# Hymba block on one core: keys turned on VectorE, one cluster for the last Gram blocks, stores and loads queued behind the weights

## The chip, the core and the metric

The kernel runs on one core of a Trainium2 chip. The metric is the device time of one execution in microseconds. A core has five engines that work side by side, each through its own list of instructions in order: TensorE (PE in the profile; its weight loads are shown apart as PEld), VectorE (DVE), ScalarE (ACT), GpSimd (POOL) and SyncE (SP). SyncE does no arithmetic here; it issues the transfers between DRAM and on-chip memory, one after the other, and a transfer that has to wait for data holds up all transfers behind it. An instruction that needs a result of another engine waits for a semaphore.

## The reference

The input `x` is 512 tokens of 2048 values in float32; 16 meta tokens stand ahead of them (528 rows in all). One layer is computed:

```
hn = rmsnorm(h);  P = hn @ w_in                       # 2048 -> 8320 columns
r, k, v, g_r, wl, al = token shift of the first 4224 columns (16 heads x 64)
decay = exp(-exp(-softplus(-(w0 + tanh(wl) @ w_lora_up)) - 0.5))
a  = sigmoid(a0 + al @ a_lora_up)
kk = k * k_k, each head's vector divided by its norm
k  = k * (1 + (a - 1) * k_a);   b = kk * a
S_t = S_{t-1} diag(decay_t) - (S_{t-1} kk_t) b_t^T + v_t k_t^T      # per head, 64 x 64
y_t = S_t r_t
y_a = (groupnorm(y) + sum(r * k * r_k) * v) * silu(g_r)
y_b = B * conv3(C * h) * silu(g_c)                     # the other 4096 columns
out = rmsnorm(h + concat(y_a, y_b) @ w_out), without the meta rows
```

## The kernel before, in words

**The projection.** Weights and activations are each split into a rounded part and a rest (`xh`, `xl`; `wh`, `wl`), and three products of them are summed (`steps`, line 315): `ps_k`, `ps_r`, `ps_v`, `ps_g`, `ps_C`, `ps_h`, `ps_B`, `ps_gc` are the groups of the profile. One tile of 128 columns ("a main") takes 16 x 3 matmuls for each of two ranges of tokens, or for all 512 tokens at once (B and gc). Weights arrive in blocks of 128 x 1024 (`wr`, three buffers, `prefetch`); ScalarE rounds each half (line 126) and VectorE, or GpSimd for the second half, forms the rest (line 127); a half is called a quarter of a main's weights here, as four make one main.

**Pairs of heads.** The 16 heads are worked in 8 pairs. The order of mains is: lora, then for each two pairs k, r, v, k, r, v, g, g, and a C, h, B, gc of the convolution; four more sets C, h, B, gc come at the end. The program of TensorE is written out by hand: `mains()` yields one projection matmul at a time, `fill(ns)` lets so many nanoseconds of them pass, `until(what, i)` all of them up to a named main, and between them stand the small matmuls of the pairs. `FW` holds the lengths of these fills. VectorE, ScalarE, GpSimd and SyncE are put in order by the tile scheduler when the kernel is built, by its own priorities (`high_priority`, `ahead()`); `issue_after` forbids a transfer to be placed ahead of a named other one.

**One pair** (`prepare(i)`): after its keys (`shift_full`, line 343) `lora_up` (lines 540 to 546) loads the pair's low-rank weights (`lur`), ScalarE rounds them (`luh`) and VectorE forms the rest (`lul`, line 545). 1062 ns of projection later `low_rank` (lines 521 and 522) multiplies by both parts, for the decay (`tz`) and for a (`ta`). From these come scaled keys `bk`, and `ar` with the scaled removal key and receptance; r is projected; after a fill (`gram` or `gram_b`) the Gram products of 9 chunks of 64 tokens follow on TensorE (line 625): eight chunks, a fill `gram2`, the ninth chunk, and 16 transposes of `bk` by TensorE (line 655) that ScalarE copies to `bt`; a fill `gram3`; then four matmuls that sum the squares of the keys (`n2`, line 666) and two that sum the bonus (`zb`, line 670). The norms go to DRAM (`sn`), as does a part of the Gram blocks (`sg`); `stash` stores the operands of the recurrence to DRAM (`opd`: `ar`, `gt`, `bt`, `vs`). `d` and `nd` are read back in another layout (line 697, 698), and VectorE inverts 72 blocks of 16 x 16 by 33 instructions (lines 701 to 734), called the solve below. The result goes to DRAM (`sx`) and comes back as `xT`, `xo` (`load_inverse`); both are put off by `later(ns, ...)`, which runs a function once so much projection has passed, behind the last weight's transfer. v follows: bonus times v is stored (`rbd`), v is turned (`vs`) and stored by 8 transfers.

**Two pairs** (`invert`): after a fill (`solve`), the inverses of 16 are joined to those of 64 on TensorE, and `xT` is stored.

**The recurrence** (`recur`): 9 chunks in turn; each loads its operands (`ct`, 16 buffers), and runs three clusters of small matmuls with fills between: `rz` (line 889), `z` and then `zs` (line 939: the change of the state) with `zy` (line 943: the outputs). It runs beside the last mains. Then `split_mix` splits what goes into the output projection (`o`, line 1070), which ends the kernel.

The lines that the change touches are 40 to 46 (`FW`), 420 (`mixd`), 540 to 546, 566, 621 to 673, 685 to 698, 749 to 757, 858 to 863, 921 and 939.

Of the kernel before, what the change touches and what calls it, by code (L numbers as in the profile page):

```python
# [40 lines left out]


FW = dict(
    evac=34, start=1062, lora=2200, gram=8000, gram_b=13500, gram2=4800, gram3=3500, misc=2000, v=2000, vt=1000, solve=22500, solve_first=26000,
    tr=3200, lev=3000, cp=4200, out=1500, begin=17000, p=2900, u=2900, s=5200, last=3700, mix=2600,
)

# [29 lines left out]
def hymba_kernel(ctx: ExitStack, tc: tile.TileContext, xt, xtok, w_in, w_out, pv, lup, cst, msk, gf, out):  # L77
# [299 lines left out]
    def use(what, i, ps):  # L377
        if what == "lora":
            use_lora(ps)
        elif what in ("k", "v"):  # L380
            t = cq.tile([P, LP], F32, tag=what, name=f"{what}{i}")
            nc.gpsimd.memset(t[:, META:CH], 0.0)
            shift_full(ps, tile_of[what] + i, f"{what}{i}", padded(t))
            got[what, i] = t
        elif what in ("r", "g"):
            t = cq.tile([P, SEQ], F32, tag=f"r{i % 2}" if what == "r" else "g", name=f"{what}{i}")
            shift_real(ps, tile_of[what] + i, f"{what}{i}", t)
            if what == "g":
                gate(t, f"r{i}")
                later(6000, lambda: nc.sync.dma_start(gated[i], t))  # L390
            got[what, i] = t
        elif what == "C":
            u = tm(f"u{i}")
            scaled(TAIL, ps, u, 14)
            got[what, i] = u
        elif what == "h":
            u = got["C", i]
            hh = tm(f"hh{i}")
            scaled(TAIL, ps, hh, 14)
            n = SEQ + 2  # L400
            nc.gpsimd.tensor_tensor(out=u[:, 0:n], in0=u[:, 0:n], in1=hh[:, 0:n], op=ALU.mult)
            cv = tp.tile([P, SEQ], F32, tag="cw", name=f"cv{i}")
            nc.scalar.activation(cv, u[:, 0:SEQ], AF.Copy, scale=col(V_CW, i))
            for j in (1, 2):
                nc.vector.scalar_tensor_tensor(
                    out=cv, in0=u[:, j : j + SEQ], scalar=col(V_CW, 8 * j + i), in1=cv, op0=ALU.mult, op1=ALU.add
                )
            got[what, i] = cv
        elif what == "B":
            cv = got["h", i]  # L410
            b = tm(f"b{i}")[:, 0:SEQ]
            scaled(REAL, ps, b, META)
            nc.gpsimd.tensor_tensor(out=cv, in0=cv, in1=b, op=ALU.mult)
        else:
            cv = got["h", i]
            g = tm(f"gc{i}")[:, 0:SEQ]
            scaled(REAL, ps, g, META)
            gate(g, f"c{i}")
            nc.vector.scalar_tensor_tensor(out=cv, in0=cv, scalar=0.5, in1=g, op0=ALU.mult, op1=ALU.mult)
            nc.sync.dma_start(mixd[8 + i], cv)  # L420
        ready.add((what, i))

    ready = set()
# [115 lines left out]
    def lora_up(i):  # L539
        raw = cq.tile([P, 2, P], F32, tag="lur", name=f"lur{i}")  # L540
        hi = cq.tile([P, 2, P], F32R, tag="luh", name=f"luh{i}")
        lo = cq.tile([P, 2, P], F32R, tag="lul", name=f"lul{i}")
        nc.sync.dma_start(raw, lup[i])
        nc.scalar.copy(hi, raw)
        nc.vector.tensor_tensor(out=lo, in0=raw, in1=hi.bitcast(F32), op=ALU.subtract)
        return hi, lo
# [17 lines left out]
        )  # L564

    def stash(i, src, o, n, row=0, rows_n=P, c0=0, cn=NCH, step=1):
        nc.sync.dma_start(spot(i, row, rows_n, c0, cn, step, o, n), src)

    def prepare(i):
        p = i % 2  # L570
# [47 lines left out]
        fill(FW["gram_b" if p else "gram"])  # L618

        gt = cq.tile([P, 2, NCH, P], F32, tag=f"gt{p}", name=f"gt{i}")  # L620
        bt = cq.tile([P, 2, NCH - 1, CH], F32, tag="bt", name=f"bt{i}")

        def gram(z, c, c0):
            for h, hs, ho in heads:
# [22 lines left out]
        masked(za, 0, 4)  # L647
        masked(zc, 4, 8)
        fill(FW["gram2"])
        ze = [pi.tile([P, 1, P], F32, tag=("misc", "ser")[h], name=f"g{i}_8_{h}") for h in range(2)]  # L650
        zz = [pz.tile([P, NCH - 1, CH], F32, tag="tz", name=f"bt{i}_{h}") for h in range(2)]
        gram(ze, 8, 8)
        for c in range(NCH - 1):
            for h, hs, ho in heads:
                nc.tensor.transpose(
                    zz[h][:, c], bk[hs, c, h : h + 2, :].rearrange("p a s -> p (a s)"),
                    ident[hs, 64 * h : 64 * h + 64],
                )
        masked(ze, 8, 9)
        for h in range(2):  # L660
            nc.scalar.copy(bt[:, h], zz[h])
        fill(FW["gram3"])
        n2 = tr(f"n2{i}")
        for j, (a, b) in enumerate(((0, 288), (288, LP))):
            z = pi.tile([2, b - a], F32, tag=("misc", "ser")[j], name=f"n2_{i}_{a}")
            nc.tensor.matmul(z, ones[:, P : P + 2], sqh[:, a:b], start=True, stop=False)
            nc.tensor.matmul(z, ones[:, P : P + 2], sql[:, a:b], start=False, stop=True)
            nc.scalar.copy(n2[0:2, a:b], z)
        zb = pz.tile([P, SEQ], F32, tag="tz", name=f"zb{i}")
        nc.tensor.matmul(zb, ones[:, 0:P], rh, start=True, stop=False)  # L670
        nc.tensor.matmul(zb, ones[:, 0:P], rl, start=False, stop=True)
        nc.scalar.copy(r, zb)
        fill(FW["misc"])

# [7 lines left out]
        def blocks(t):  # L682
            return bass.AP(tensor=t.tensor, offset=t.offset, ap=[[BLK, 8 * NCH], [CH, 16], [1, 16]])

        nc.sync.dma_start(
            bass.AP(tensor=sn.tensor, offset=sn.offset, ap=[[CH, 2], [P, NCH], [1, CH]]), c3(n2[0:2])
        )
        for h in range(2):
            nc.sync.dma_start(rows(sg, h), gt[64 * h : 64 * h + 64, h, :, 0:CH])
        NB = 8 * NCH  # L690
        d = cq.tile([NB, 256], F32, tag="d", name=f"d{i}").rearrange("p (s t) -> p s t", t=16)
        stash(i, ar.rearrange("p c a s -> p c (a s)"), O_AR, 2 * CH)
# [1 line left out]
            stash(i, gt[ho, h], O_KK, 2 * CH, 64 * h, 64)  # L694
            stash(i, gt[hs, h, :, CH:P], O_BR, CH, 64 * h, 64)
        nd = cq.tile([NB, 16], F32, tag="nd", name=f"nd{i}")
        nc.sync.dma_start(d, blocks(sg))
        nc.sync.dma_start(nd, sn.rearrange("(p s) -> p s", s=16))
        y = cq.tile([NB, 256], F32, tag="y", name=f"y{i}").rearrange("p (s t) -> p s t", t=16)
        nc.gpsimd.memset(y, 0.0)  # L700
        nc.vector.tensor_scalar(out=nd, in0=nd, scalar1=1e-24, scalar2=None, op0=ALU.max)
# [44 lines left out]
                    ),  # L746
                )

        later(13500 if p else 29000, lambda: nc.sync.dma_start(blocks(sx), y))
        later(16500 if p else 33000, load_inverse)  # L750

        for h, hs, ho in heads:
            stash(i, bt[hs, h], O_B, CH, 64 * h, 64, 0, NCH - 1)
            stash(i, bt[ho, h], O_K, CH, 64 * h, 64, 0, NCH - 1)
        until("v", i)
        v = got["v", i]
        nc.vector.tensor_tensor(out=r, in0=r, in1=v[:, CH:LP], op=ALU.mult)
        nc.sync.dma_start(rbd[i], r)
        fill(FW["v"])

        vs = cq.tile([P, NCH, CH], F32, tag="vs", name=f"vs{i}")
# [10 lines left out]
    def invert(two):  # L772
# [81 lines left out]
        for q in both:  # L854
            for e in range(2):
                for h, lo, hi in quads:
                    nc.vector.tensor_copy(two[q]["xT"][lo, 2 - e : NCH : 2, 32:CH], z[e][lo, q])
        for t in two:
            if t["i"] % 2 == 0:
                stash(t["i"], t["xT"], O_X, CH)  # L860
            else:
                for h, hs, ho in heads:
                    stash(t["i"], t["xT"][hs], O_X, CH, 64 - 64 * h, 64)
        fill(FW["out"] if first < NPAIR - 2 else FW["begin"])

    def load_chunk(ch, c, pairs, ops):
# [8 lines left out]
    def recur(ch):  # L875
# [4 lines left out]
        for c in range(NCH):  # L880
# [36 lines left out]
            for k in range(4):  # L917
                for e in range(2):
                    t, j = ops[c, 2 * k + e], 4 * e + k
                    if not last:  # L920
                        here += [(zs, j, t, O_B, u[:, e, k], 0, 2), (zs, j, t, O_K, t[:, O_V : O_V + CH], 1, 2)]
                    if c and j < NPAIR - 1:
                        there += [
                            (zy, j, st[:, j], O_AR + CH, t, 0, 3),
                            (zy, j, t[:, O_V : O_V + CH], O_KK + CH, t, 1, 3),
                            (zy, j, u[:, e, k], O_BR, t, 2, 3),
                        ]
                    elif c:

                        here += [  # L930
                            (z[0][:, 0], 0, t, O_AR + CH, st[:, j], 0, 3),
                            (z[0][:, 0], 0, t, O_KK + CH, t[:, O_V : O_V + CH], 1, 3),
                            (z[0][:, 0], 0, t, O_BR, u[:, e, k], 2, 3),
                        ]
            for n in range(max(len(here), len(there))):
                if n < len(here):
                    d, j, t, o, x, a, b = here[n]
                    for h, hs, ho in heads:
                        nc.tensor.matmul(d[hs, j], t[hs, o : o + CH], x[hs], start=(a == 0), stop=(a == b - 1))  # L939
                if n < len(there):  # L940
                    d, j, x, o, t, a, b = there[n]
                    for h, hs, ho in heads:
# [52 lines left out]
    for i in range(0, NPAIR, 2):  # L995
        invert([prepare(i), prepare(i + 1)])
    until("g", NPAIR - 1)
    ph2.close()
    with tc.tile_pool(name="ch", bufs=1, side="right", reuse_waits="tile") as ch:
        recur(ch)  # L1000
# [34 lines left out]
    for j in range(NPAIR + 4, KT):  # L1035
        while ("gc", j - NPAIR) not in ready:
            step()
        split_mix(j)
    for _ in flow:
        pass  # L1040
# [194 lines left out]
```

## Time and profile before

| | |
|---|---|
| time, median of 3 runs | 1055.89 us (1055.82 to 1059.58) |
| the profiled execution | 1054.6 us |
| its span in the trace | 1052.8 us |
| mean granted TensorE clock | 0.996 |
| TensorE busy, 9973 matmuls | 1034.8 us (98%) |
| its weight loads | 945.1 us (90%) |
| VectorE | 566.4 us (54%) |
| ScalarE | 365.9 us (35%) |
| GpSimd | 308.3 us (29%) |
| DRAM traffic | read 129.05 MB, written 36.88 MB, 158 GB/s |
| transfers of operands to DRAM | `ar` 8, `gt` 16, `bt` 32, weights of the projection 127 |

A group's row reads: line, engine, operation, output<-inputs, shape, number, then busy time and mean length in ns, then the idle time of that engine just before these instructions and which instruction ended it. A row of the timeline begins with the start and the length in us; square brackets give the idle time ahead of it and what ended it. A row of the chain of waits gives start, length, engine, what it worked on and the line. A row of the windows gives the stretch, its length and the busy time of TensorE, its weight loads, VectorE, ScalarE, GpSimd, then the granted TensorE clock, the share of the transfer engines, and GB/s. Matmuls are pipelined, so the lengths of neighbours overlap.

### The profile page before, as it was taken

How to read it: one execution, taken by the hardware profiler on the slowest of the kernel's cores; microseconds unless marked ns; L12 is line 12 of the kernel's file. 1: busy time of each engine (PE TensorE's matmuls, PEld its weight loads, DVE VectorE, ACT ScalarE, POOL GpSimd, SP SyncE). 2: the span in 40 equal slices, each digit the busy share in tenths (PEclk: the TensorE clock that was granted, in tenths of full speed). 3: DMA queues.
4: the chain of work that ended last, by engine and by line, in shares of the span. 5: the costliest groups of instructions: out<-in, count | busy, mean ns of one | idle time of the engine just before them, and what ended most of it. 6: DMA issues, size and time to landing. Idle time of an engine off the chain costs nothing.

```text
span 1052.8 us, 23986 instructions
## 1 busy us (share of the span) xinstructions
PE 1034.8 (98%) x9973; PEld 945.1 (90%) x9973; DVE 566.4 (54%) x1072; ACT 365.9 (35%) x682; POOL 308.3 (29%) x315
## 2 busy tenths in 40 slices
PE   7999999999999999999999999999999999999996
PEld 6999998999998999989999989888898988888885
DVE  6774965559563658653757642455454781212132
ACT  7543422433332433233443232222222342323232
POOL 0132413324222323132323231323233242424232
PEclk9999999999999999999999999999999999999999
DMA  8446475364854363753364748778654978322314
GB/s 297 135 124 155 121 175 142 108 153 120 197 152 115 108 164 112 175 155 114 104 170 127 178 129 291 232 214 248 181 146 112 275 233 302 98 87 95 100 61 160
DMA packets 182893, 167.49 MB, mean 159 GB/s; under 512 B 120960, under 2 KB 143232, under 8 KB 182400
## 3 DMA queue, kind: packets, MB, share of 16 engines
q1 hardware_dynamic: 182208, 164.90, 53.7%
q8 instruction: 78, 1.28, 0.5%
q10 hardware_dynamic: 576, 1.07, 0.3%
q14 instruction: 31, 0.25, 0.1%
HBM read 129.05 MB, written 36.88 MB: 158 GB/s over the span
## 4 chain that ended last, share of the span: by engine, by line
PE 90%; DVE 4%; issue 2%; DMA 1%; ACT 1%; POOL 1%; SPq 0%; DVEq 0%; ACTq 0%; POOLq 0%
PE o L1070 17%; PE ps_g L315 9%; PE ps_gc L315 9%; PE ps_k L315 9%; PE ps_B L315 8%; PE ps_h L315 8%; PE ps_C L315 8%; PE ps_r L315 7%; PE ps_v L315 7%; PE g L625 2%; PE zs L939 1%; PE ps_lora L315 1%; PE rz L889 1%; PE zy L943 1%; DMA wq<-in_w_in_dram 1%
## 5 line engine op out<-in xcount | busy, mean ns | idle before, releaser
L127 POOL TENSOR_TENSOR wl<-wr,wh 128x512 fp32r<-128x512 f32 x150 | 211.2, 1410 | 456.2 <-ACT wh L126 423.2
L126 ACT CAST wh<-wr 128x512 fp32r<-128x512 f32 x312 | 188.7, 619 | 385.2 <-PE o L1070 92.2
L127 DVE TENSOR_TENSOR wl<-wr,wh 128x512 fp32r<-128x512 f32 x162 | 124.8, 775 | 241.4 <-ACT wh L126 236.0
L1070 PE MATMUL o<-wh,m 128*128 128x512 f32 (+1 forms) x484 | 145.3, 384 | 0.0
L1070 PEld LDWEIGHTS o<-wh,m 128*128 128x128 f32 x484 | 89.6, 188 | 21.3
L1070 PE MATMUL o<-wl,m 128*128 128x512 f32 (+1 forms) x242 | 92.6, 389 | 0.0
L315 PE MATMUL ps_k<-xl,wh 128*128 128x264 f32 x256 | 73.2, 286 | 0.0
L315 PE MATMUL ps_g<-xh,wl 128*128 128x258 f32 (+1 forms) x256 | 72.2, 282 | 0.9 <-DVE wl L127 0.8
L315 PE MATMUL ps_v<-xh,wh 128*128 128x264 f32 x256 | 73.1, 286 | 0.0
L315 PE MATMUL ps_k<-xh,wh 128*128 128x264 f32 x256 | 73.0, 285 | 0.0
L315 PE MATMUL ps_r<-xh,wh 128*128 128x258 f32 (+1 forms) x256 | 72.2, 282 | 0.7 <-ACT wh L225 0.7
L315 PE MATMUL ps_h<-xh,wl 128*128 128x258 f32 (+1 forms) x256 | 72.8, 285 | 0.0
L315 PE MATMUL ps_k<-xh,wl 128*128 128x264 f32 x256 | 72.7, 284 | 0.0
L315 PE MATMUL ps_v<-xh,wl 128*128 128x264 f32 x256 | 72.7, 284 | 0.0
L315 PE MATMUL ps_v<-xl,wh 128*128 128x264 f32 x256 | 72.7, 284 | 0.0
L315 PE MATMUL ps_g<-xl,wh 128*128 128x258 f32 (+1 forms) x256 | 72.4, 283 | 0.0
L315 PE MATMUL ps_h<-xh,wh 128*128 128x258 f32 (+1 forms) x256 | 72.3, 282 | 0.0
L315 PE MATMUL ps_g<-xh,wh 128*128 128x258 f32 (+1 forms) x256 | 72.3, 282 | 0.0
L315 PE MATMUL ps_C<-xh,wh 128*128 128x258 f32 (+1 forms) x256 | 72.3, 282 | 0.0
L315 PE MATMUL ps_C<-xh,wl 128*128 128x258 f32 (+1 forms) x256 | 72.3, 282 | 0.0
L315 PE MATMUL ps_r<-xl,wh 128*128 128x258 f32 (+1 forms) x256 | 72.1, 282 | 0.0
L315 PE MATMUL ps_h<-xl,wh 128*128 128x258 f32 (+1 forms) x256 | 72.1, 282 | 0.0
(271 smaller groups left out, 2705.9 us busy)
## 6 DMA issues: line engine op xcount, KB each, us to landing
wr<-in_w_in_dram SPq DMA_DIRECT2D x127, 512.0 KB
ct<-opd SPq DMA_DIRECT2D x64, 288.0 KB
wr<-in_w_out_dram SPq DMA_DIRECT2D x32, 512.0 KB
opd<-ar SPq DMA_DIRECT2D x8, 576.0 KB
opd<-gt SPq DMA_DIRECT2D x16, 288.0 KB
opd<-bt SPq DMA_DIRECT2D x32, 128.0 KB
xres<-in_xtok_dram SPq DMA_DIRECT2D x4, 768.0 KB
out_dram<-xres SPq DMA_DIRECT2D x6, 512.0 KB
```

Of the source, the lines that this page charges most:

```text
L126: nc.scalar.copy(hi, rq)
L127: eng.tensor_tensor(out=lo, in0=rq, in1=hi.bitcast(F32), op=ALU.subtract)
L315: nc.tensor.matmul(ps[r], ww[:, w], xx[:, kt, a:b], start=(kt == 0 and n == 0), stop=(kt == KT - 1 and n == 2))
L625: nc.tensor.matmul(z[h][:, c - c0], bk[hs, c, h : h + 2, :].rearrange("p a s -> p (a s)"), ar[hs, c].rearrange("p a s -> p (a s)"), start= ...
L889: nc.tensor.matmul(z[e][ho if e else hs, 0, k], t[hs, o : o + CH], t[hs, O_V : O_V + CH] if part else st[hs, 4 * e + k], start=(part == 0 ...
L939: nc.tensor.matmul(d[hs, j], t[hs, o : o + CH], x[hs], start=(a == 0), stop=(a == b - 1))
L943: nc.tensor.matmul(d[ho, j], t[hs, o : o + CH], x[hs], start=(a == 0), stop=(a == b - 1))
L1070: nc.tensor.matmul(ps[t + p], mm[:, tk], ww[:, o], start=(jj == 0 and q == 0), stop=(jj == KT - 1 and q == 2))
```

## The change

In words, in the order of the code:

- `FW`: `gram2` becomes 5500, `gram3` goes.
- `behind(dst, src)` is new: a transfer that SyncE may not issue ahead of the last weight transfer written so far. The low-rank weights `lur`, all of `stash`, the stores `sn`, `sg` and `rbd` and the loads `d` and `nd` use it.
- The scaled keys are turned by two VectorE transposes in blocks of 32 x 32, ahead of the Gram products, in place of 16 on TensorE and two copies by ScalarE. In `bt`, and so in DRAM and in the loaded `ct`, b and key now alternate element by element, and 8 transfers of a pair store them in place of 4.
- The ninth chunk's Gram products, the key norms (512 and 64 columns in place of 288 and 288) and the bonus sums stand in one cluster on TensorE with no fill between; the evacuations of the first two get the `ahead()` priority.
- The store of the 16 x 16 inverses of odd pairs is put off by 21000 in place of 13500, its load by 24000 in place of 16500; the store of the joined inverse by 4500 and that of the convolution's result (`mixd`) by 6000, both new.
- The recurrence reads b and key, as TensorE weights, at every second element.
- What is still put off is run ahead of the recurrence and in the loop of the last mixing tiles.

```diff
-    ... gram=8000, gram_b=13500, gram2=4800, gram3=3500, misc=2000, ...
+    ... gram=8000, gram_b=13500, gram2=5500, misc=2000, ...
@@ use
-            nc.sync.dma_start(mixd[8 + i], cv)
+            later(6000, lambda: nc.sync.dma_start(mixd[8 + i], cv))
@@ lora_up
-        nc.sync.dma_start(raw, lup[i])
+        behind(raw, lup[i])
@@ stash
-        nc.sync.dma_start(spot(i, row, rows_n, c0, cn, step, o, n), src)
+        behind(spot(i, row, rows_n, c0, cn, step, o, n), src)
+
+    def behind(dst, src):
+        with tc.issue_after(state["dma"]):
+            nc.sync.dma_start(dst, src)
@@ prepare
-        bt = cq.tile([P, 2, NCH - 1, CH], F32, tag="bt", name=f"bt{i}")
+        bt = cq.tile([P, NCH - 1, 2, CH // 2, 2], F32, tag="bt", name=f"bt{i}")
+        for a in range(2):
+            nc.vector.transpose(bt[:, :, :, :, a], bk[:, 0 : NCH - 1, a].rearrange("p c (t s) -> p c t s", t=2))
...
-        ze = [pi.tile([P, 1, P], F32, tag=("misc", "ser")[h], name=f"g{i}_8_{h}") for h in range(2)]
-        zz = [pz.tile([P, NCH - 1, CH], F32, tag="tz", name=f"bt{i}_{h}") for h in range(2)]
-        gram(ze, 8, 8)
-        for c in range(NCH - 1):
-            for h, hs, ho in heads:
-                nc.tensor.transpose(
-                    zz[h][:, c], bk[hs, c, h : h + 2, :].rearrange("p a s -> p (a s)"),
-                    ident[hs, 64 * h : 64 * h + 64],
-                )
-        masked(ze, 8, 9)
-        for h in range(2):
-            nc.scalar.copy(bt[:, h], zz[h])
-        fill(FW["gram3"])
+        ze = [pz.tile([P, P + CH], F32, tag="tz", name=f"g{i}_8_{h}") for h in range(2)]
+        gram([z[:, 0:P].unsqueeze(1) for z in ze], 8, 8)
         n2 = tr(f"n2{i}")
-        for j, (a, b) in enumerate(((0, 288), (288, LP))):
-            z = pi.tile([2, b - a], F32, tag=("misc", "ser")[j], name=f"n2_{i}_{a}")
+        zn = pi.tile([2, SEQ], F32, tag="misc", name=f"n2_{i}")
+        zs = ((zn, 0, SEQ), (ze[0][0:2, P : P + CH], SEQ, LP))
+        for z, a, b in zs:
             nc.tensor.matmul(z, ones[:, P : P + 2], sqh[:, a:b], start=True, stop=False)
             nc.tensor.matmul(z, ones[:, P : P + 2], sql[:, a:b], start=False, stop=True)
-            nc.scalar.copy(n2[0:2, a:b], z)
-        zb = pz.tile([P, SEQ], F32, tag="tz", name=f"zb{i}")
+        zb = pi.tile([P, SEQ], F32, tag="ser", name=f"zb{i}")
         nc.tensor.matmul(zb, ones[:, 0:P], rh, start=True, stop=False)
         nc.tensor.matmul(zb, ones[:, 0:P], rl, start=False, stop=True)
+        with ahead():
+            for z, a, b in zs:
+                nc.scalar.copy(n2[0:2, a:b], z)
+            masked([z[:, 0:P].unsqueeze(1) for z in ze], 8, 9)
...
-        later(13500 if p else 29000, lambda: nc.sync.dma_start(blocks(sx), y))
-        later(16500 if p else 33000, load_inverse)
+        later(21000 if p else 29000, lambda: nc.sync.dma_start(blocks(sx), y))
+        later(24000 if p else 33000, load_inverse)
         for h, hs, ho in heads:
-            stash(i, bt[hs, h], O_B, CH, 64 * h, 64, 0, NCH - 1)
-            stash(i, bt[ho, h], O_K, CH, 64 * h, 64, 0, NCH - 1)
+            for b in range(2):
+                for t in range(2):
+                    stash(
+                        i, bt[64 * h + 32 * b : 64 * h + 32 * b + 32, :, t].rearrange("p c s a -> p c (s a)"),
+                        O_B + 64 * b, 64, 64 * h + 32 * t, 32, 0, NCH - 1,
+                    )
@@ invert
+        def put_inverse():
...
+        later(4500, put_inverse)
@@ recur
-                        here += [(zs, j, t, O_B, u[:, e, k], 0, 2), (zs, j, t, O_K, t[:, O_V : O_V + CH], 1, 2)]
+                        bb = t[:, O_B : O_B + 2 * CH].rearrange("p (s a) -> p a s", a=2)
+                        here += [(zs, j, bb[:, 0], 0, u[:, e, k], 0, 2), (zs, j, bb[:, 1], 0, t[:, O_V : O_V + CH], 1, 2)]
...
```

The stores `sn`, `sg`, `rbd` and the loads `d`, `nd` go through `behind` in the same way as `lur`.

More of the change, by code (lines that the diff above doesn't have):

```diff
@@ L43 @@
 FW = dict(
-    evac=34, start=1062, lora=2200, gram=8000, gram_b=13500, gram2=4800, gram3=3500, misc=2000, v=2000, vt=1000, solve=22500, solve_first=26000,
+    evac=34, start=1062, lora=2200, gram=8000, gram_b=13500, gram2=5500, misc=2000, v=2000, vt=1000, solve=22500, solve_first=26000,
     tr=3200, lev=3000, cp=4200, out=1500, begin=17000, p=2900, u=2900, s=5200, last=3700, mix=2600,
@@ L683, in blocks @@
             return bass.AP(tensor=t.tensor, offset=t.offset, ap=[[BLK, 8 * NCH], [CH, 16], [1, 16]])
-        nc.sync.dma_start(
+        behind(
             bass.AP(tensor=sn.tensor, offset=sn.offset, ap=[[CH, 2], [P, NCH], [1, CH]]), c3(n2[0:2])
@@ L688, in prepare @@
         for h in range(2):
-            nc.sync.dma_start(rows(sg, h), gt[64 * h : 64 * h + 64, h, :, 0:CH])
+            behind(rows(sg, h), gt[64 * h : 64 * h + 64, h, :, 0:CH])
         NB = 8 * NCH
@@ L696, in prepare @@
         nd = cq.tile([NB, 16], F32, tag="nd", name=f"nd{i}")
-        nc.sync.dma_start(d, blocks(sg))
-        nc.sync.dma_start(nd, sn.rearrange("(p s) -> p s", s=16))
+        behind(d, blocks(sg))
+        behind(nd, sn.rearrange("(p s) -> p s", s=16))
         y = cq.tile([NB, 256], F32, tag="y", name=f"y{i}").rearrange("p (s t) -> p s t", t=16)
@@ L757, in prepare @@
         nc.vector.tensor_tensor(out=r, in0=r, in1=v[:, CH:LP], op=ALU.mult)
-        nc.sync.dma_start(rbd[i], r)
+        behind(rbd[i], r)
         fill(FW["v"])
@@ L857, in invert @@
                     nc.vector.tensor_copy(two[q]["xT"][lo, 2 - e : NCH : 2, 32:CH], z[e][lo, q])
[L858 to L863, printed above, removed]
+        def put_inverse():
+            for t in two:
+                if t["i"] % 2 == 0:
+                    stash(t["i"], t["xT"], O_X, CH)
+                else:
+                    for h, hs, ho in heads:
+                        stash(t["i"], t["xT"][hs], O_X, CH, 64 - 64 * h, 64)
+        later(4500, put_inverse)
         fill(FW["out"] if first < NPAIR - 2 else FW["begin"])
@@ L938, in recur @@
                     for h, hs, ho in heads:
-                        nc.tensor.matmul(d[hs, j], t[hs, o : o + CH], x[hs], start=(a == 0), stop=(a == b - 1))
+                        w = t[hs, o : o + CH] if o else t[hs]
+                        nc.tensor.matmul(d[hs, j], w, x[hs], start=(a == 0), stop=(a == b - 1))
                 if n < len(there):
@@ L997, in hymba_kernel @@
     until("g", NPAIR - 1)
+    run_pending(float("inf"))
     ph2.close()
@@ L1037, in hymba_kernel @@
             step()
+        run_pending(float("inf"))
         split_mix(j)
```

## The prediction

> **What bounds the kernel now.** I read the page first, then TensorE's groups by line, the chain of waits, and the timelines of one pair of heads.
>
> ```profile
> span 1052.8 us, 23986 instructions
> PE 1034.8 (98%) x9973; PEld 945.1 (90%) x9973; DVE 566.4 (54%) x1072; ACT 365.9 (35%) x682; POOL 308.3 (29%) x315
> PE 90%; DVE 4%; issue 2%; DMA 1%; ACT 1%; POOL 1%; SPq 0%; DVEq 0%; ACTq 0%; POOLq 0%
> ```
>
> ```profile
> L315 PE MATMUL ps_g<-xh,wl 128*128 128x258 f32 (+1 forms) x256 | 72.2, 282 | 0.9 <-DVE wl L127 0.8
> L315 PE MATMUL ps_B<-xh,wl 128*128 128x512 f32 x128 | 50.8, 397 | 0.9 <-DVE wl L127 0.9
> ```
>
> TensorE is the bound, in a fixed instruction order, with next to no idle time behind its first tens of microseconds: these two groups lost 1.7 us to weights that VectorE had not split. So the change can gain little more than the TensorE work it removes, and every new wait of TensorE is paid in full. What a wait costs beyond itself stands in two stretches of the windows (the number behind POOL's is the granted clock): after the stop-and-go of the start TensorE ran 3.5 us at 0.53, losing 3.5 x 0.47 = 1.6 us.
>
> ```profile
> 21.50:25.00 3.50, 3.50 (x17) 3.50 (x18) 3.40 (x6) 3.50 (x7) 0.00 (x0) 0.53 0.93 339
> 25.00:60.00 35.00, 35.00 (x291) 34.77 (x290) 25.31 (x47) 20.17 (x38) 5.04 (x10) 1.00 0.38 123
> ```
>
> **The change part by part. TensorE's own work.** The timeline at pair 2's last chunk, then pieces of the chain:
>
> ```profile
> 220.46 0.49 PE L625 MATMUL g<-ar,bk 64*128 64x128 f32 x4
> 220.79 0.66 PE L655 MATMUL bt<-cs,bk 64*128 64x64 f32 x16
> 221.38 0.39 PE L315 MATMUL ps_k<-xl,wh 128*128 128x264 f32 x1
> ```
>
> ```profile
> 87.52 0.13 PE n L666
> 88.05 0.24 PE zb L670
> 89.93 5.34 PE ps_v L315 x44
> ```
>
> The 16 transposes hold TensorE from 220.79 to 221.38: 0.59 us, times 8 pairs, 4.7 us gone. The key norms were four matmuls of 288 columns at 0.13 (0.52); they become two of 512, priced as zb's at 0.24, and two of 64, which this trace lacks for this type. Between 0.02 and 0.13 I take 0.06: 0.60, so +0.6 us in eight pairs. The sum, -4.1. The two 576-wide copies of keys by ScalarE and their PSUM banks go; two VectorE turns of about 0.7 come (the xn turns of 128x512 below are the nearest row), 11 us in all on an engine at 54%, behind operands needed only for stores: nothing, unless VectorE is late anyway.
>
> **Weights of the recurrence read at every second element.** No operation here reads TensorE weights so.
>
> ```profile
> 657.80 0.28 PE L939 MATMUL zs<-ct 64*64 64x64 f32 x4
> 657.92 0.28 PE L939 MATMUL zs<-u,ct 64*64 64x64 f32 x4
> ```
>
> A step of four records takes 0.117 us, and 16 steps in 8 chunks read such weights. If the load sets the pace and halves, 128 x 0.117 = 15 us; if not, nothing; no row suggests a gain. I take nothing. [...]
>
> **The low-rank weights, requested behind the projection's.** `lora_up` loads the pair's low-rank weights; ScalarE rounds them (luh) and VectorE forms the rest (lul). Before, that load stands early on SP's queue, and lul follows as soon as the pair before has used its own (243.61, below, is pair 4's). In the changed program's order lul of pairs 1, 3, 5, 7 stands behind the whole 16x16 solve of the pair before. Pair 3, with the number in VectorE's and in SP's order:
>
> ```
> VectorE 297, 298  L343 k_3106 (keys of pair 3)
> VectorE 299 to 331  L703 nd_2991 ... L736 y_2994 (solve of pair 2, 33 instructions)
> VectorE 332  L545 lul_3134<-lur_3132,luh_3133
> TensorE 1729  L522 tz_0_3150<-la,lul_3134 [waits VectorE]
> SP 142 to 155: d, nd, 2 of bt, rbd, 8 of vs, a weight, L571 lur_3132
> ```
>
> On VectorE and TensorE all of this is in order. TensorE reaches that matmul soon after the keys' projection, which the change leaves so (`start` is still 1062). Rows of before for the same place, then the solve of an odd pair, which ran nearly alone:
>
> ```profile
> 232.00 1.31 PE ps_r L315 x11
> 233.44 0.12 PE tz L522
> ```
>
> ```profile
> 233.28 1.38 DVE L343 SCALAR_TENSOR_TENSOR k<-pr_k,omm,sh_k 128x16 f32<-128x16 f32 x2 [0.81 <-ACT sh_k L341]
> 243.61 0.42 DVE L545 TENSOR_TENSOR lul<-lur,luh 128x256 fp32r<-128x256 f32 x1
> ```
>
> ```profile
> 282.75 0.16 DVE L701 TENSOR_SCALAR nd<-nd 72x16 f32<-72x16 f32 x1
> 282.94 0.25 DVE L702 RECIPROCAL nd<-nd 72x16 f32<-72x16 f32 x1
> 283.75 0.43 DVE L334 TENSOR_TENSOR pr_g<-ps_g,rs 128x256 f32<-128x256 f32 x1 [0.24 <-PE ps_g L315]
> 284.37 0.71 DVE L785 STREAM_TRANSPOSE xn<-xT 128x512 f32<-128x512 f32 x1
> 285.74 0.16 DVE L734 TENSOR_REDUCE y<-prod 72x4 f32<-72x8 f32 x1
> 293.46 0.68 DVE L734 TENSOR_REDUCE y<-prod 72x64 f32<-72x512 f32 x1
> ```
>
> The last 25 instructions of the solve run from 285.74 to 294.14, 8.4 us; the eight ahead of them start about 0.2 apart, 1.6: a solve is 10.0. The keys end at 234.66 (233.28 + 1.38), so lul ends at 234.66 + 10.0 + 0.42 = 245.1, and TensorE, there at 233.44, waits 11.6 us. Pairs 3, 5, 7: 34.8. For pair 1 the last work ahead of the solve is r:
>
> ```profile
> 91.19 1.27 DVE L352 SCALAR_TENSOR_TENSOR r<-pr_r,omm,sh_r 128x512 f32<-128x512 f32 x1 [0.79 <-ACT sh_r L351]
> ```
>
> It ended 2.5 behind the projection's end (89.93); the solve and lul add 10.4, and in the changed order 22 matmuls (5.34 / 44 each, 2.7) lie between that end and the wait: 10.2. Sum of the four: +45.0.
>
> This holds if nd (the norms, back from DRAM) and the low-rank load are in time:
>
> ```profile
> 138.41 1.00 SPq L698 DMA_DIRECT2D nd<-sn  x1
> 229.93 2.09 SPq L698 DMA_DIRECT2D nd<-sn  x1
> 232.06 2.64 SPq L567 DMA_DIRECT2D opd<-bt  x4
> 235.43 3.62 SPq L567 DMA_DIRECT2D opd<-vs  x7
> ```
>
> ```profile
> 142.06 0.98 DVE L701 TENSOR_SCALAR nd<-nd 72x16 f32<-72x16 f32 x1 [0.53 <-DMA nd<-sn]
> ```
>
> Pair 1's nd was used 2.7 us behind its issue (139.4 to 142.1). The changed order puts the norms with the last Gram block, three to four microseconds earlier, but six key stores go ahead of the Gram stores, already ready by then: nd issued at some 229 lands near 232, ahead of 234.66. Behind it SP has 2 of bt, rbd, 8 of vs and a weight, 12 at 0.5 to 0.66: lur goes at about 236 and lands near 240, still under the solve's cover. Were both late by 4 us, each wait would be so much longer; below 10 it can hardly fall, since solve and lul alone are 10.4 and the keys' 2.66 exceed TensorE's 1.44. Each wait also costs clock: 4 x 1.6 = 6.4 (0 to 6.8).
>
> **B's first weights in the first two pairs.** Before, the split that stood behind h's evacuation was the third quarter's; now VectorE 225 to 227 are cv, cv and wl_1893, the first quarter's, and ScalarE rounds it behind cv too.
>
> ```profile
> 152.31 0.39 PE L315 MATMUL ps_B<-xh,wh 128*128 128x512 f32 x1
> 154.05 1.30 POOL L401 TENSOR_TENSOR u<-u,hh 128x514 f32<-128x514 f32 x1 [11.04 <-DVE hh L334]
> 156.14 1.54 DVE L405 SCALAR_TENSOR_TENSOR cv<-u,pvt,cv 128x512 f32<-128x512 f32 x2 [2.17 <-ACT cv L403]
> 159.43 0.50 PE L315 MATMUL ps_B<-xh,wl 128*128 128x512 f32 x1 [0.94 <-DVE wl L127]
> ```
>
> The split ended between 158.3 and 159.4, 6.0 to 7.1 behind B's start; the first quarter needs it two matmuls behind that start, some 0.5. Of the wait, 5.5 to 6.6, I take the middle, 6.0, less the 0.94 that was paid: +5.1 (0 to 6).
>
> **A split within the solve.** In pairs 3, 5, 7 a weight split for C's third quarter stands behind 25 of the odd solve's instructions, next to the key-turn xn. From g's end (283.72): 0.5 evacuation, 5.5 of solve and xn, 0.7 split, 6.7, against 6.0 of TensorE: +0.8 each, +2.4 (0 to 6). Inverse load, stores of the inverse, mixd and the shorter `gram2`: behind `later`, and at the recurrence's start mixd still stands between the ct loads: 0 (-1 to 3). The weights requested first take away the 0.8 of ps_g, behind the pairs' new waits: -0.8.
>
> **Sum**, on the profiled execution's 1054.6: -4.1 - 0.8 + 45.0 + 6.4 + 5.1 + 2.4 = +54.0, 1108.6. It lies 1.3 under the median (1055.89); I give 1108.
>
> **Rivals.** *Faster*: TensorE does not wait for lul, because the solve of the pair before is over by then. It decides where lul starts: ahead of 233.4 TensorE loses nothing. For it speaks that pair 2's last Gram block ends at 221, so that nd could land before the keys; against it that VectorE keeps its order and takes the keys (297, 298) ahead of the solve, so that an early nd does not help: it needs another order on the chip than the built one. Then -4.1 - 0.8: 1050. *SP is later*: the extra stores delay nd or lur by 4 us; SP's rows of 0.5 to 0.66 per store speak for slips, the slack of 2.7 against: 4 x 4 more, 1124. *Strided weights cost*: 1123; nothing in the trace speaks for or against. *Half of it*: the four waits are cut short since TensorE's order gives VectorE other cover, or the clock stays: 4 x 6, without B's: 1075. [...]
>
> **How the numbers follow.** The likeliest, 1108, has 0.70; SP later 0.09; strided weights 0.08; half of it 0.07; faster 0.05; the remaining 0.01 no change. The waits at 10 each without clock and without B's give 1086; 13.5 each with B's at 6 and C's at 6 give 1122, and the two dearer rivals reach past 1124: 1084 to 1130. Slower by over 0.5%, the size that a measurement of this kernel tells from none, has 0.94.
>
> **What would show it.** Four waits of TensorE at tz (L522) for VectorE's lul, 10 to 13 us each, a granted clock near 0.5 behind each; a wait of some 5 at ps_B of the first pairs; no bt on TensorE; zs steps still 0.117. Wrong if TensorE's group tz shows no idle time before it, or if zs steps are near 0.2.

## The result, and the profile after

The changed kernel takes 1118.97 us (median of 4 runs, 1118.85 to 1119.51) against 1055.86 us before: 1.0577 times as long, 95% interval 1.0547 to 1.0608, 63 us more. The profiled execution took 1119.01 us with a span of 1117.2, 64.4 above the span before; the differences below are made between these two profiled executions.

The head of the page of the changed kernel, then TensorE's waits (columns: who waited, for whom; us in total, times, the longest):

```profile
span 1117.2 us, 23763 instructions
PE 1046.6 (94%) x9845; PEld 952.3 (85%) x9845; DVE 581.4 (52%) x1088; ACT 359.4 (32%) x666; POOL 299.3 (27%) x315
```

```profile
PE tz L521 <- ACT luh L544: 39.1, 4, 10.4
PE ps_C L315 <- DVE wl L127: 7.3, 3, 2.5
PE tz L522 <- DVE lul L545: 4.5, 4, 1.5
PE ps_B L315 <- ACT wh L126: 3.1, 1, 3.1
PE ps_B L315 <- DVE wl L127: 2.0, 1, 2.0
```

The page says two things at once. TensorE has 128 matmuls fewer and is nevertheless busy 11.8 us longer: part of its work ran at a lower clock (granted 0.967 on average, 0.996 before). And its share of the span fell from 98% to 94%: 56.0 us of waits stand in these five rows, where the kernel before had 1.7 at B and g. Pair 3, the place that the prediction worked out, in the timeline of the changed kernel:

```profile
251.50 0.80 SPq L571 DMA_DIRECT2D opd<-bt  x2
252.41 0.45 SPq L571 DMA_DIRECT2D rbd<-r  x1
252.91 3.98 SPq L571 DMA_DIRECT2D opd<-vs  x8
253.62 1.36 DVE L343 SCALAR_TENSOR_TENSOR k<-pr_k,omm,sh_k 128x16 f32<-128x16 f32 x2 [0.81 <-ACT sh_k L341]
254.90 0.16 DVE L703 TENSOR_SCALAR nd<-nd 72x16 f32<-72x16 f32 x1
256.98 0.40 SPq L134 DMA_DIRECT2D wr<-in_w_in_dram  x1
257.43 0.43 SPq L571 DMA_DIRECT2D lur<-in_lup_dram  x1
262.57 0.40 ACT L544 CAST luh<-lur 128x256 fp32r<-128x256 f32 x1 [8.99 <-DMA lur<-in_lup_dram]
263.03 0.59 PE L521 MATMUL tz<-la,luh 128*128 128x272 f32 x1 [9.37 <-ACT luh L544]
264.04 0.68 DVE L736 TENSOR_REDUCE y<-prod 72x64 f32<-72x512 f32 x1
264.64 0.41 DVE L545 TENSOR_TENSOR lul<-lur,luh 128x256 fp32r<-128x256 f32 x1
265.11 0.59 PE L522 MATMUL tz<-la,lul 128*128 128x272 f32 x1 [1.49 <-DVE lul L545]
```

The solve runs on VectorE from 254.90 to 264.72, and lul follows it, as the prediction had it. The transfer is the part it had earlier: `lur` is issued at 257.43, behind two key stores, the bonus, eight `vs` stores and a weight, and lands at 262.57, two us ahead of the solve's end. TensorE's first matmul there (L521) waits for the transfer, and the second (L522) for the rest of the solve.

The granted clock (the number behind POOL's) was low in five stretches, one at B's two waits and one at each of the four waits at tz. The windows, cut where it fell and rose: B's, pair 3's, and the sum and mean of all five:

```profile
170.63:177.46 6.83, 5.09 (x12) 4.03 (x13) 5.24 (x5) 2.17 (x4) 4.81 (x4) 0.50 0.56 147
255.96:269.61 13.65, 5.10 (x22) 4.79 (x23) 8.78 (x30) 1.66 (x4) 0.00 (x0) 0.50 0.52 137
sum 61.43, PE 24.93 PEld 22.64 DVE 40.69 ACT 8.81 POOL 4.81; mean PE 4.99 PEld 4.53 DVE 8.14 ACT 1.76 POOL 0.96
```

TensorE (PE) was busy for 24.9 us of them, at half the clock: 24.9 x 0.50 = 12.5 us lost, 2.4 to 2.6 in each.

**The account.** Waits: 43.6 at tz, 7.3 at C, 5.1 at B, less the 1.7 of before, +54.3. Clock +12.5. TensorE's work: transposes -4.7, norms +0.3 (the chain has 0.33 + 0.23 for a pair's four matmuls in place of 4 x 0.13). Sum +62.4 of 64.4. Another 1.5 us were lost by 30 us already, ahead of most of what the change touches: at the start the clock was at 0.50 for 6.8 us here, and for 3.4 in the execution before. The last 0.5 I did not place.

### The profile page after: what moved, and what is told of

It reads as the page before. It is cut to its first block, busy times and chain, and to the rows that moved or that the text cites. A ratio compares the mean times of both kernels' runs of the same rounds, so it can differ in the third digit from the quotient of the medians.

```text
span 1117.2 us, 23763 instructions
## 1 busy us (share of the span) xinstructions
PE 1046.6 (94%) x9845; PEld 952.3 (85%) x9845; DVE 581.4 (52%) x1088; ACT 359.4 (32%) x666; POOL 299.3 (27%) x315
## 5 line engine op out<-in xcount | busy, mean ns | idle before, releaser
L127 POOL TENSOR_TENSOR wl<-wr,wh 128x512 fp32r<-128x512 f32 x150 | 203.4, 1357 | 482.3 <-ACT wh L126 475.2
L315 PE MATMUL ps_r<-xh,wh 128*128 128x258 f32 (+1 forms) x256 | 74.7, 292 | 0.3 <-ACT wh L225 0.3
L315 PE MATMUL ps_r<-xh,wl 128*128 128x258 f32 (+1 forms) x256 | 74.9, 292 | 0.0
L315 PE MATMUL ps_r<-xl,wh 128*128 128x258 f32 (+1 forms) x256 | 74.4, 291 | 0.0
L315 PE MATMUL ps_C<-xl,wh 128*128 128x258 f32 (+1 forms) x256 | 72.3, 282 | 0.0
```

The lines of the kernel that those rows point to most:

```text
L127: eng.tensor_tensor(out=lo, in0=rq, in1=hi.bitcast(F32), op=ALU.subtract)
L315: nc.tensor.matmul(ps[r], ww[:, w], xx[:, kt, a:b], start=(kt == 0 and n == 0), stop=(kt == KT - 1 and n == 2))
```

## The experiments

All ratios are to the kernel before, timed on the same chip beside it, with 95% intervals. Times of the kernel before were 1055.5 to 1056.9.

### Which late link makes the waits at tz

Two things became late together: the transfer of `lur` (behind the weights on SyncE), and the place of lul (behind the solve on VectorE). Three runs take them apart.

```diff
 e1_lur_plain, on the changed kernel
-        behind(raw, lup[i])
+        nc.sync.dma_start(raw, lup[i])
 e2_lul_pool, on the changed kernel
-        nc.vector.tensor_tensor(out=lo, in0=raw, in1=hi.bitcast(F32), op=ALU.subtract)
+        nc.gpsimd.tensor_tensor(out=lo, in0=raw, in1=hi.bitcast(F32), op=ALU.subtract)
 e3_lul_behind_solve: as e1, and
+        with tc.issue_after(state["solved"]):   # the last instruction of the solve before
             nc.vector.tensor_tensor(out=lo, ...)
```

> The changed kernel, with the low-rank load alone as before (no longer behind the last weight). My theory, that the four waits at tz (39.1 + 4.5 us) and the slow clock behind each (the windows behind one show 1.75 + 0.5 us lost) come from this load's late place and nothing else: they go, 43.6 + 4 x 2.2 = 52 us less than 1119, 1067. The waits of C (7.3) and of B (5.1) stay. Rival: the stores behind the weights hold up something else that these waits covered; then a new wait of TensorE appears and the time stays above 1085.

> The changed kernel, with the rest lul formed by GpSimd in place of VectorE; the load stays behind the weights. It takes the solve's place on VectorE out of the matter and leaves the transfer's. If the transfer alone suffices (it landed at 262.6 in pair 3, TensorE was there at 253.7): each wait is shortened only by the 1.1 to 1.5 that TensorE waited for lul beyond luh, 3 to 5 in all, 1114 to 1116. If the solve's place on VectorE was the cause, as my prediction told it, the waits fall to a few us: below 1080.

> The changed kernel, with the low-rank load as early as before, and lul held behind the last instruction of the solve of the pair before on VectorE. It leaves the order on VectorE of the changed kernel and takes the late transfer away. If that order alone suffices: four waits, now for lul and not for luh, of 10 to 11 us each, and 1114 to 1119. If the late transfer was what the waits needed: near 1067.

Measured: e1 1094.39 us (1.0354, 1.0339 to 1.0370), which misses the 1067 and lies in the rival's range; e2 1117.79 (1.0576, 1.0556 to 1.0595), a little above the 1114 to 1116 of the transfer's case and far from the other; e3 1118.62 (1.0574, 1.0548 to 1.0600), in the range of the order's case. TensorE's waits of e2:

```profile
PE tz L521 <- ACT luh L544: 39.2, 4, 10.5
PE tz L522 <- POOL lul L545: 3.3, 4, 1.2
```

of e3:

```profile
PE tz L522 <- DVE lul L546: 45.8, 4, 11.8
```

Either link alone makes the waits. With lul off VectorE altogether, the late transfer holds TensorE as long; with the transfer early, the place behind the solve does, for 11.3 us at pairs 3, 5 and 7 (the prediction has 11.6) and 11.8 at pair 1 (it has 10.2). So the prediction named a sufficient cause, and not the only one: taking lul out of the solve's way alone, as someone might who had read only it, brought 1 us less of waits (42.5) and no time that can be told from none (1.0576 against 1.0577).

e1, with both links mended, ends the waits at tz but not the loss. Its TensorE waits:

```profile
PE ps_C L315 <- DVE wl L127: 19.5, 3, 6.6
PE ps_v L315 <- DVE wl L127: 7.0, 3, 3.0
PE ps_B L315 <- ACT wh L126: 3.1, 1, 3.1
PE ps_B L315 <- DVE wl L127: 1.9, 1, 1.9
```

43.6 us of waits went, and 12.2 more appeared at C and 7.0 at v: the rival's outcome. Whether the stores make them, as the rival has it, e5 and e11 show.

### The load behind the weights by itself

```diff
 e4_before_lur_behind, on the kernel before
-        nc.sync.dma_start(raw, lup[i])
+        with tc.issue_after(state["dma"]):
+            nc.sync.dma_start(raw, lup[i])
```

> The kernel before, with nothing changed but the low-rank load behind the last weight. In its built order lul of pair 1 stands behind pair 0's solve, those of pairs 3, 5, 7 ahead of the solve, with the load right behind a weight and ahead of the stores. By the theory that place in the orders decides: one wait of about 10 at pair 1 and 2 of clock, 1068, and none at the other three. Rival, that the load behind the weights costs a wait by itself: four waits, 1100 and more.

Measured: 1067.13 us (1.0099, 1.0083 to 1.0115), as forecast, with one place of waiting at tz, pair 1:

```profile
PE tz L521 <- ACT luh L545: 5.0, 1, 5.0
PE tz L522 <- DVE lul L546: 4.2, 1, 4.2
```

The same edit makes 9.2 us of waits here, and the changed kernel has 43.6 at the same place, because the scheduler puts lul and the load elsewhere. At pairs 3, 5, 7 the load is issued right behind a weight and ahead of the pair's stores, lul stands ahead of the solve, and no wait follows. The price is that of the built order, and not one that the edit has everywhere.

### The cluster, and the stores and due times

```diff
 e5_cluster_only: the kernel before with the VectorE turns, the alternating layout, the cluster and gram2=5500;
 all transfers plain, due times as before
 e6_before_stores_later: the kernel before with stash, sn, sg, d, nd, rbd behind the weights, and
-        later(13500 if p else 29000, ...)   later(16500 if p else 33000, load_inverse)
+        later(21000 if p else 29000, ...)   later(24000 if p else 33000, load_inverse)
 and the later mixd and put_inverse; no cluster, lur early
 e10_before_later: the kernel before with the later sx, load_inverse and mixd alone
 e11_before_stores: the kernel before with the stores and loads behind the weights alone
```

> The kernel before with the TensorE part of the change alone: the turns by VectorE with the alternating layout, the one cluster, gram2 at 5500; no transfer behind the weights, none put off longer. The run with the early low-rank load showed new waits at C's third-quarter weights (19.5 us in 3) and v's (7.0 in 3). Theory: the cluster makes the solve ready earlier for the scheduler, which then puts these splits behind the solve on VectorE; then the cluster alone has them too: 1090 to 1098. Rival: they come from the stores behind the weights; then this is 4 below the kernel before, 1052.

> The kernel before with all stores, norms and Gram loads behind the weights and all the later due times of the change, but not the low-rank load and not the cluster. By the theory above no weight split stands in a solve in its built order, and it costs nothing: 1054 to 1058. By the rival, some 26 us of waits and their clock: 1085 and more.

> The kernel before with only the later due times (store and load of the 16 x 16 inverses of odd pairs, the convolution's result). The run with stores behind and later due times had 5.8 us of waits at t for the turned inverse (xn). If the due times are their cause: the same three waits of about 2 us, 1060 to 1066. If the stores behind the weights are: 1055 to 1057.

> The kernel before with only stash, norms, Gram stores and loads and the bonus behind the weights. If the due times cause the waits at t, this has none: 1054 to 1060, with the 2.9 us of ps_g that the run with both showed. If the stores do: 1062 to 1068.

Measured: e5 1086.36 (1.0291, 1.0276 to 1.0307), somewhat below the forecast; e6 1068.66 (1.0120, 1.0105 to 1.0135), a miss of both theories; e10 1065.68 (1.0097, 1.0074 to 1.0121) and e11 1057.82 (1.0019, 1.0010 to 1.0028), both as forecast if the due times cause the waits at t. The waits of e5:

```profile
PE ps_C L315 <- DVE wl L127: 13.9, 3, 4.8
PE ps_v L315 <- POOL wl L127: 6.2, 3, 2.1
PE ps_B L315 <- ACT wh L126: 3.1, 1, 3.1
```

of e10:

```profile
PE t L792 <- DVE xn L785: 6.8, 3, 2.8
```

So the TensorE part of the change, which takes 4.4 us of work away, costs 31 us by itself; no run takes its pieces (turns, layout, cluster, fill) apart. In its built VectorE order the third-quarter split of C stands at 404 with the odd pair's solve at 373 to 407, and v's at 339 with the even pair's solve at 300 to 347; in the kernel before no such split stands in a solve from pair 2 on. At C that place is what TensorE waits for. At v it is not in this run: VectorE's split ended at 256.33 in pair 2, and TensorE waited from 260.5 to 262.6. The row of v's waits names GpSimd, whose split of the other half of the block took 6.57 us there (as long at pairs 4 and 6), where 1.29 is the median of the changed kernel's 150, beside a VectorE that worked without a pause on the solve and on r:

```profile
255.97 6.57 POOL L127 TENSOR_TENSOR wl<-wr,wh 128x512 fp32r<-128x512 f32 x1 [3.34 <-ACT wh L126]
```

The later due times cost some 10 us alone: the inverses of the odd pairs come back too late for the joining on TensorE (t), three waits, 6.8 in all and 2.8 the longest, and a granted clock of 0.990 over the profiled execution, against 0.996 before. In the changed kernel no wait at t shows, presumably as TensorE's other waits leave the inverses more time; of the runs with these due times below only e8 has one. The stores behind the weights cost 2 (e11) and show no wait at C or v, which e5 has without them: the rival of e1 is out as a cause.

The stretch in the changed kernel where C waits, VectorE and GpSimd by time:

```profile
318.91 1.29 POOL L127 TENSOR_TENSOR wl<-wr,wh 128x512 fp32r<-128x512 f32 x1 [11.08 <-ACT wh L126]
322.21 1.26 POOL L127 TENSOR_TENSOR wl<-wr,wh 128x512 fp32r<-128x512 f32 x1 [2.00 <-PE ps_C L315]
```

```profile
316.56 0.42 DVE L334 TENSOR_TENSOR pr_g<-ps_g,rs 128x256 f32<-128x256 f32 x1 [0.97 <-PE ps_g L315]
316.90 0.16 DVE L703 TENSOR_SCALAR nd<-nd 72x16 f32<-72x16 f32 x1
318.98 0.16 DVE L736 TENSOR_REDUCE y<-prod 72x4 f32<-72x8 f32 x1
319.17 1.05 DVE L721 TENSOR_TENSOR prod<-d,y 72x8 f32<-72x8 f32 x1
321.62 0.16 DVE L721 TENSOR_TENSOR prod<-d,y 72x8 f32<-72x8 f32 x1
322.40 1.19 DVE L721 TENSOR_TENSOR prod<-d,y 72x64 f32<-72x64 f32 x1
324.05 0.68 DVE L127 TENSOR_TENSOR wl<-wr,wh 128x512 fp32r<-128x512 f32 x1
```

The same product takes 0.16 us at 321.62 and 1.05 at 319.17, where it ends at 320.22 with GpSimd's split (320.20); the larger one at 322.40 takes 1.19, where the next of its size takes 0.27, and ends at 323.59, a little behind GpSimd's (323.47). These two stretched instructions hold 0.9 us each, 1.8 of the 2.4 that TensorE waits for this split.

### Undoing the places one by one

```diff
 e7_splits_on_gpsimd, on e1
-                    split_w(..., nc.gpsimd if q and j > 8 else nc.vector)
+                    split_w(..., nc.gpsimd if (q and j > 8) or (q == 0 and j in by_pool) else nc.vector)
     by_pool: third quarters of C 1, 2, 3 and of v 2, 4, 6
 e8_and_b_first: as e7, and in use("h", 0)
+                    es.enter_context(tc.issue_after(state["cast", 4 * plan.index(("B", 0))]))
                 nc.scalar.activation(cv, u[:, 0:SEQ], AF.Copy, scale=col(V_CW, i))
 e9_cluster_splits_moved: e5 with the same edit at B, and by_pool:
     third quarters of C 1, 2, 3 and v 3, 5, 7; first of h 1, 2, 3; first and third of g 2, 4, 6
 e12_solve_fill: as e9, and
-    solve=22500
+    solve=25500
```

> The changed kernel with the low-rank load as before, and six weight splits (third quarters of C in sets 1 to 3, of v in pairs 2, 4, 6) formed by GpSimd in place of VectorE, so that none stands behind a solve. Against the run with the early load alone (1094): the 26.5 us of waits of C and v go, with 6 stretches of slow clock of 1.5 to 2: 1056 to 1060. If these splits were late for another reason than the solve, GpSimd waits as long and it stays near 1094.

> As the one before, and B's first weights of set 0 are rounded ahead of cv on ScalarE, and split ahead of it on VectorE. That takes most of B's 5.0 us and 2.5 of slow clock: some 6 to 7 less than the one before, 1049 to 1053, which would be 3 to 6 below the kernel before: the TensorE work saved (4.1), at last visible.

Measured: e7 1077.89 (1.0211, 1.0194 to 1.0228), e8 1073.94 (1.0176, 1.0158 to 1.0195): both forecasts missed. The C waits went, but h's first split, the next one behind the same solve, took over. The v splits that I had moved were those of the wrong pairs: the waits are in 3, 5, 7. And with B's first weights ahead of cv, B waits 0.7 (4.6 in e7), but the joining of the first two pairs then waits 4.5 for xn. TensorE's waits of e8:

```profile
PE ps_v L316 <- DVE wl L128: 6.9, 3, 3.0
PE ps_h L316 <- DVE wl L128: 6.8, 3, 2.4
PE t L802 <- DVE xn L795: 4.5, 1, 4.5
PE ps_B L316 <- DVE wl L128: 0.7, 1, 0.7
```

> The kernel with the TensorE part alone (1086.4), and every weight split that stood behind an odd or even solve from pair 2 on (C's third quarters, v's third quarters of pairs 3, 5, 7, h's first, g's first and third of pairs 2, 4, 6) formed by GpSimd, B's first weights of set 0 rounded and split ahead of cv. Theory: all of the 24.7 us of waits at C, v and B were these places; then it is the kernel before less the TensorE work saved (4.1) and its own waits at B and g (1.7), and slow clock none: 1049 to 1053. Rival: the waits go on to the next split or the next evacuation, as they did when six splits were moved (h took over 6.9 us): 1060 or more.

> As the run with all these splits moved (1063.8), and the fill solve at 25500 in place of 22500: the cluster takes a fill away ahead of the inverse, and TensorE came to t 2.1 to 2.5 us before xn was there, three times. The waits at t (6.7) go with three stretches of slow clock (windows of 8 to 12 us at 0.79 to 0.86, some 1.7 each): 6.7 + 5 = 12 less, 1052, 4 below the kernel before. Rival: xn comes later by as much, since the store of the inverses waits for the same flow; then it stays at 1060 and more.

Measured: e9 1063.75 (1.0080, 1.0064 to 1.0095), a miss by the rival's case: no split waits for a solve any more, but t does, as the cluster took a fill away ahead of the joining. e12 1051.12 (0.9942, 0.9926 to 0.9958), as forecast: faster than the kernel before by 0.6%. The waits of e9; in e12 the first of these rows is gone, and the other two are the same:

```profile
PE t L801 <- DVE xn L794: 6.7, 3, 2.5
PE ps_v L316 <- POOL wl L128: 2.7, 3, 0.9
PE ps_B L316 <- DVE wl L128: 0.7, 1, 0.7
```

One number changed between them, three microseconds of projection ahead of the joining. With the 6.7 us of waits went three stretches of 3.4 us at a clock of 0.50, which had cost 5.0, as the forecast had it: 11.7 of the 13.5 by which the span got shorter. No run has the same moved splits in the kernel before, so a part of the 0.6% may be theirs and not the change's.

## Why the prediction was right, point by point

- **Direction and size.** +54.0 forecast, +64.4 between the profiled executions; 1108 against 1119, inside 1084 to 1130. The chief term was right: four waits at tz, +45.0 forecast, 43.6 measured, 10.9 at pairs 3, 5 and 7 (11.6 forecast) and 11.1 at pair 1 (10.2).
- **The cause of that term** was told as the solve on VectorE, with the load landing under its cover. It landed two us before the cover ended, not five, and e2 shows that it would have held TensorE as long alone. The first half of the mechanism is confirmed by e3; the prediction's view that the load was harmless is not. The sign that it gave, 10 to 13 us for lul at L522, did not come so: 39.1 of the 43.6 stand at L521, for the load, though lul ended each of the four waits, as forecast.
- **Clock**, mis-sized: 1.6 for each of four waits, 6.4; measured 2.4 to 2.6 for each and 2.5 behind B's waits, 12.5. The row of the start that it was taken from had a stretch of 3.5 us at 0.53; here the clock falls within the wait and stays at 0.50 until 4.2 to 4.5 us behind its end. The sum had no clock behind B's waits; the trace shows that they paid as well, 2.5.
- **C's split in the odd solve**, mis-sized: 2.4 forecast, 7.3 measured. Its 6.7 from g's end to the split's end became 8.2 (316.5 to 324.7), since two instructions of the solve took 1.05 and 1.19 us, in place of 0.16 and 0.27, beside GpSimd's splits; TensorE was there after 5.9, where 6.0 was forecast. With the load early, the built order puts the split behind nearly the whole solve (406 of 373 to 407, against 397 of 372 to 406 in the changed kernel), and it is 6.5 per pair (e1).
- **B's first weights**: a wait of 6.0 forecast, of which 0.94 was paid before, +5.1; measured a wait of 5.1 (3.1 for ScalarE's rounding, 2.0 for the rest), +4.2.
- **TensorE's work**: -4.1 forecast, -4.4 measured; but e5 shows the real price of that part, +31 by the orders that it brings about. The prediction found two places of it, B's and C's, and did not see that this part was their cause.
- **Strided weights at nothing**: right, and the rival of 15 us is out. Before, then after:

```profile
L939 PE MATMUL zs<-ct x256: 218/218/218, 657.8 to 780.9; 64*64 64x64 f32 x128
```

```profile
L951 PE MATMUL zs<-ct x256: 219/220/224, 720.4 to 842.5; 64*64 64x64 f32 x128
L951 PEld LDWEIGHTS zs<-ct x256: 134/135/142, 720.3 to 842.5; 64*64 64x64 f32 x128
```

  Shortest, median and longest length in ns: 220 against 218, with a weight load of 135 as for the contiguous ones (135 before and after). The trace before had no row for the zero in the sum; these rows show 2 ns more for a matmul, and no more for a weight load.
- **Later due times at nothing**: not seen in the changed kernel, but wrong as a price of the edit, 10 us alone (e10).

## What to carry to other kernels

Where a scheduler orders an engine that works in order, the price of an edit is the price of the order it brings about: read, in the built order, what stands ahead of each operand that the bottleneck engine will ask for, and look for long dependent chains (here 33 small instructions, 10 us) in front of short urgent ones. Mending the largest wait need not give it back: the order shifts with each edit, and a wait of the bottleneck hides those behind it (t waits in e8 and e9 only once B's and C's waits are gone). e1 gave back 25 of 52 us, and the splits at C, v, h, g and B and the fill ahead of t had to follow until the 4 us of work that the change saves could be seen. A wait's price is the wait and, where the clock fell behind it, that clock: 2.4 to 2.6 us more at each wait at tz here, nothing at the three of 2.4 to 2.5 at C.

## What the runs showed of the hardware

- **The length of a wait did not decide alone whether the clock fell.** A wait of 2.2 us at h in e7 (ended at 303.4) was followed by a clock of 0.50, one of 2.0 at v in e1 (ended at 258.5) likewise; three waits of 2.4 to 2.5 at C in the changed kernel were followed by 1.00, and so was one of 1.95 at v in e7 (ended at 256.4). At v in e5, two waits of 2.1 went apart: 0.53 in the 2 us behind the one that ended at 262.6, 1.00 behind the one that ended at 423.7. In the trace of the changed kernel the low stretches of the start, of B and of tz begin at 20.44, 95.54, 170.63, 255.96, 423.22 and 590.47, whole multiples of 3.41 us apart, and last 6.83 or 13.65 us, two or four times 3.41. Windows of that length, e1 at v and the changed kernel at its last wait at C:

```profile
255.08:258.49 3.41, 1.46 (x13) 1.25 (x11) 3.41 (x6) 0.64 (x3) 1.75 (x2) 1.00 0.00 0
258.49:261.90 3.41, 3.40 (x15) 3.40 (x16) 3.41 (x6) 2.14 (x5) 3.41 (x1) 0.50 0.02 7
```

```profile
655.31:658.73 3.42, 1.68 (x15) 1.47 (x13) 3.04 (x12) 1.14 (x2) 1.27 (x1) 1.00 0.28 115
658.73:662.14 3.41, 2.63 (x22) 2.63 (x23) 3.20 (x9) 0.00 (x0) 0.00 (x0) 1.00 0.47 121
```

  In e1 the whole wait lies in one window, and TensorE was busy for 1.46 us of it, a share of 0.43; in the changed kernel two windows share the wait, with 0.49 and 0.77. With the changed kernel's trace cut into such windows, from 25 us to 30 us before the end, each of the five full-clock windows with a share of 0.21 to 0.36 was followed by a low one, and none of those with 0.47 and more was, the three at C's waits with 0.47 to 0.49 among them. A low window was followed by another one at shares from 0.00 to 0.50, and by the full clock at 1.00. These are the counts of one trace; what decides at other shares stays open.
- **Some VectorE products beside GpSimd's splits, and some of the splits, took longer.** The rows above at 319.17 and 322.40 show it for VectorE, 1.05 us in place of 0.16 and 1.19 in place of 0.27, each ending within 0.12 us of the split beside it; the split of 6.57 us in e5, against the median of 1.29, for GpSimd, with VectorE busy throughout TensorE's wait there (2.40 of 2.40 us). What held them up, no run takes apart.
